# Reordering the projections of a gated-delta mixer and shrinking the fill-in products of the last expert group

## The chip, the core and the metric

The kernel runs on one core of a Trainium2 chip. The metric is the device time of one execution in microseconds; lower is better. The core has five engines that run side by side, each in its own instruction order: PE (TensorE, matrix products), DVE (VectorE), ACT (ScalarE), POOL (GpSimd) and SP (which here issues the loads). An instruction that must wait holds up everything behind it on its engine.

## The reference, cut to what matters

Two model blocks follow each other on 256 tokens of width 1024, in float32. The first block doesn't change here. The second has a mixer and a layer of 64 experts:

```python
def hybrid_mixer(h, ...):                       # h: 16 meta tokens and 256 tokens
    proj = rms_norm_2(h, norm_g) @ w_in
    f_in, qkv, z, ab, gate_f, gate_d = split(proj)
    y_f = fft_mix(f_in) @ w_fourier
    q, k, v = split(silu(depthwise_conv_centred(qkv, conv_w)))     # 5 taps
    q, k = l2_normalize(q), l2_normalize(k)
    o = gated_delta_chunked(q, k, v, g_f, beta_f) + flipped(gated_delta_chunked(flipped ...))
    y_d = (rms_norm_2(o) * silu(z)) @ w_delta
    return (sigmoid(gate_f) * y_f + sigmoid(gate_d) * y_d) @ w_out

def gated_delta_chunked(q, k, v, g, beta):      # per head and chunk
    a_mat = strict_lower(k_beta @ k.T * decay)
    t_mat = inverse(eye + a_mat)                # unit lower triangular
    u, w = t_mat @ (v * beta), t_mat @ (k_beta * exp(g))
    # then a scan over the chunks with a state

def hierarchical_moe(h, ...):                   # 64 experts, 2 per token
    y = (silu(x @ w_gate[e]) * (x @ w_up[e])) @ w_down[e]
```

## The kernel before, in words

**Projections.** Every 128 output features of a projection are one tile: a 512 KB load of float32 weights (`wraw`), a rounded copy `whi` on ACT (L293), the remainder `wlo` on POOL in two halves (L298), and 24 products on PE (`dense_fm`, L333, L334 and L338) into one of four PSUM banks. Then the tile's own `use` function empties the bank. For keys, queries and values it is the convolution (`conv`): a copy on ACT (L1007), four multiply-adds on DVE (L1011), a tanh on ACT (L1013), and a last multiply-add on DVE (L1014). For the gate `gd` it is one tanh on ACT (L1030), for `z` a tanh on ACT (L1038) and one DVE operation (L1039).

**Queue.** The tiles stand in a list, `queue`, in the order in which they were appended: k, q, v, gd, z, f, gf, and `wfo`, eight tiles each for most of them. `fill(n)` emits the next n tiles; `need(label)` emits until none of that label is left.

**Serial work.** Beside the tiles runs the mixer's chain, as generators: `keys` (norms of the keys), `products` (matrices of keys with keys and with queries) beside `meta`, `substitution` (31 dependent steps on DVE that invert 32x32 triangles, L1385 and L1386), `merges` (small products that join the inverted triangles to 128x128), and `scan`. `values` transposes v (L1405, L1406), then makes the start state of the forward scan out of the meta tokens (L1409 to L1425). `weave(gens, per)` steps each generator once, at high priority, then emits `per` tiles. A scheduler with a model of the engines' times then fixes the order on each engine.

```python
weave([products(), meta()], W2)          # 1.3 tiles a round
need("v")
prefetch(NFIX, wst["raw"])               # the first two expert chunks
weave([values(), substitution()], W3)    # 1.0
weave([merges()], W4)                    # 1.0
need("z")
weave([q_factors(), scan(1), scan(0)], W5)
```

**Experts.** The expert weights are 192 chunks of 1 MB, 12 for each of 16 groups of four experts: 8 for gate and up (`gate`, L1783), 4 for down (`down`, L1822). 24 buffers (`slots`) take them; most are tiles of the mixer that have died, so the loads (L888) begin for real when the mixer ends, and a buffer is loaded again as soon as its chunk is used. `combine` (L1836) adds a down product into the result. In the last group, 15, `gate` issues after each chunk one more product of 512 columns that nobody reads (`psidle`, L1786), and `down` one after each of its first three chunks (L1828).

Of the kernel before, what the change touches and what calls it, by code (L numbers as in the profile page):

```python
# [217 lines left out]
def body(ctx, tc, A, out, dbg=None, stage=9):  # L218
# [644 lines left out]
    with b2:  # L863
# [158 lines left out]
        conv("q", 0, NM - 2)  # L1022
        conv("v", 16)

# [16 lines left out]
        for a in range(8):  # L1041
            dense("z", a, NM, use_z)


# [303 lines left out]
        weave([products(), meta()], W2)  # L1348
        need("v")
        prefetch(NFIX, wst["raw"])  # L1350
# [43 lines left out]

        def values():
            G.memset(OT, 0.0)
            for r0 in (0, 64):
                G.memset(Vff[r0 + 32:r0 + 64, F_, r0:r0 + 32], 0.0)
            G.memset(Vff[hi64, F_, lo64], 0.0)
            yield  # L1400
            vm = bp.tile([P, P], F32, name="vm", tag="dm")
            for t in range(2):
# [23 lines left out]

        weave([values(), substitution()], W3)

# [79 lines left out]

        weave([merges()], W4)
        need("z")  # L1510

# [216 lines left out]
    with b3:  # L1728
# [20 lines left out]
        class Four:  # L1749
# [24 lines left out]
            def gate(self, ws, busy=False):  # L1774
                self.ws = ws
                if busy:
                    idle = bank("psidle")
                gu = bank("psgu")
                for k in range(8):
                    if k % 2 == 0:  # L1780
                        self.gather(k // 2 + 2)
                    for q in range(4):
                        PE.matmul(gu[32 * q:32 * q + 32, :], self.xg[:, k, 32 * q:32 * q + 32],  # L1783
                                  ws[k][:, 512 * q:512 * q + 512], start=k == 0, stop=k == 7)
                    if self.g == 15 and busy:
                        PE.matmul(idle, ones, ws[k][:, :512], start=True, stop=True)  # L1786
                a_ = self.act = gp_.tile([P, 256], F32, name="act", bufs=GBUF["act"])
                SC.activation(a_, gu[:, :256], AF.Tanh, scale=0.5)  # L1788
                V.scalar_tensor_tensor(a_, a_, 1.0, gu[:, :256], op0=ALU.add, op1=ALU.mult)  # L1789
                V.scalar_tensor_tensor(a_, a_, 0.5, gu[:, 256:], op0=ALU.mult, op1=ALU.mult)  # L1790
# [23 lines left out]
            def down(self, c, alone=False):  # L1814
# [11 lines left out]
                if self.g == 15 and not alone and c < 3 and BUSY:  # L1826

                    PE.matmul(bank("psidle"), ones, self.ws[8 + c][:, :512], start=True, stop=True)  # L1828
                yh, yl = self.y = [gp_.tile([P, 256], F32R, name=n, bufs=GBUF["y"]) for n in ("yh", "yl")]
# [204 lines left out]
```

## Time and profile before

| | us |
|---|---|
| median of 3 runs | 1176.04 (1172.8 to 1182.49) |
| the profiled execution, its own time | 1175.15 |
| its span from first to last instruction | 1173.4 |
| PE busy in the span | 1056.8 (90%) |
| DVE busy | 545.7 (47%) |
| ACT busy | 437.8 (37%) |
| POOL busy | 426.6 (36%) |

The span falls into the first block (to about 390 us), the mixer (to about 725 us) and the experts (the rest). "Busy" on PE counts waiting inside a pipelined group too, so a full PE row says that the engine had work at hand, not that it ran at its peak. The granted clock of TensorE is given as a share of 2.4 GHz: 1.0 is 2.4 GHz, 0.5 is 1.2 GHz.

### The profile page before, as it was taken

Reading aid. Unit: us, or ns where it says so; the run is one execution under the profiler, and the core shown is the slowest. Engines: PE = TensorE matmul, PEld = TensorE weight load, DVE = VectorE, ACT = ScalarE, POOL = GpSimd, SP = SyncE. Lnnn points to the kernel's source line nnn. Section 1 sums busy time; section 2 is a strip of 40 time slices with the busy share of each in tenths; the row PEclk is TensorE's granted clock in tenths of the full one; section 3 lists DMA queues with packets and bytes.
Section 4 is the critical chain, followed back from the end, with each engine's and each line's share of the span. In section 5 each row is a group of like instructions: output and inputs, shape, how many; then the busy total and the mean of one; then the engine's idle time right before and its main releaser. Section 6 shows DMA issues by size and latency. Waiting matters only on the chain. (4 is left out here: it accounts for less than half of the span.)

```text
span 1173.4 us, 21448 instructions
## 1 busy us (share of the span) xinstructions
PE 1056.8 (90%) x8800; PEld 849.1 (72%) x8800; DVE 545.7 (47%) x1202; ACT 437.8 (37%) x753; POOL 426.6 (36%) x347
## 2 busy tenths in 40 slices
PE   7899999999999979799999999899878778877794
PEld 7899999999998879699999997454424333334351
DVE  5967546433346897885345874222211111112112
ACT  5555435444448455455423553121211111111112
POOL 4565325567773675778545651000000000000100
PEclk9999999999999989899899999999978887888888
DMA  7454434555554323253228798999999999999993
GB/s 285 160 178 160 144 108 168 192 180 180 192 204 163 124 108 108 73 192 145 73 73 316 286 347 325 422 419 421 420 421 420 420 420 420 422 420 421 420 420 118
DMA packets 58858, 307.69 MB, mean 262 GB/s; under 512 B 5984, under 2 KB 7264, under 8 KB 33280
## 3 DMA queue, kind: packets, MB, share of 16 engines
q1 hardware_dynamic: 56528, 301.59, 65.9%
q10 hardware_dynamic: 2224, 4.65, 1.1%
q8 instruction: 71, 1.16, 0.4%
q14 instruction: 35, 0.29, 0.1%
HBM read 304.12 MB, written 2.10 MB: 261 GB/s over the span
## 5 line engine op out<-in xcount | busy, mean ns | idle before, releaser
L298 POOL TENSOR_TENSOR wlo<-wraw,whi 128x512 fp32r<-128x512 f32 x230 | 325.3, 1437 | 233.8 <-ACT whi L293 104.4
L333 PE MATMUL psd<-hTh,whi 128*128 128x256 f32 (+2 forms) x1096 | 275.6, 290 | 5.6 <-ACT whi L293 4.6
L334 PE MATMUL psd<-hTl,whi 128*128 128x256 f32 (+2 forms) x1096 | 274.7, 288 | 2.0 <-DVE hTl L450 1.9
L293 ACT ACTIVATE whi<-wraw 128x1024 fp32r<-128x1024 f32 (+1 forms) x183 | 193.4, 1064 | 200.7 <-PE psd L334 109.1
L333 PEld LDWEIGHTS psd<-hTh,whi 128*128 128x128 f32 x1096 | 210.4, 192 | 8.0 <-ACT whi L293 5.0
L334 PEld LDWEIGHTS psd<-hTl,whi 128*128 128x128 f32 x1096 | 210.9, 193 | 4.4 <-DVE hTl L450 2.8
L1783 PE MATMUL psgu<-wexp,xg 128*32 128x512 f32 x1024 | 146.0, 659 | 41.6 <-DMA wexp<-in_wex_dram 41.5
L338 PE MATMUL psd<-hTh,wlo 128*128 128x256 f32 (+2 forms) x1096 | 159.7, 292 | 0.0
L338 PEld LDWEIGHTS psd<-hTh,wlo 128*128 128x128 f32 x1096 | 145.6, 197 | 1.1 <-issue 0.5
L1971 POOL TENSOR_SCALAR wexp<-cst,gcol 128x128 f32<-128x128 f32 x8 | 4.7, 603 | 387.1 <-PE psgu L1783 387.1
L298 DVE TENSOR_TENSOR wlo<-wraw,whi 128x1024 fp32r<-128x1024 f32 (+1 forms) x68 | 99.7, 1472 | 81.9 <-PE psd L338 61.9
L1783 PEld LDWEIGHTS psgu<-wexp,xg 128*32 128x32 f32 x1024 | 24.8, 112 | 118.2 <-DMA wexp<-in_wex_dram 86.4
L1822 PE MATMUL psy<-wexp,at 128*32 128x256 f32 x1024 | 78.0, 412 | 9.8 <-DVE at L1812 9.2
L1769 PEld LDWEIGHTS psg<-pm,x 128*128 128x128 f32 x512 | 73.6, 223 | 16.6 <-issue 12.0
L1769 PE MATMUL psg<-pm,x 128*128 128x128 f32 x512 | 81.7, 314 | 0.0
L1831 DVE SCALAR_TENSOR_TENSOR yl<-psy,ww,yh 128x256 fp32r<-128x256 f32 x64 | 31.0, 484 | 105.9 <-ACT yh L1830 100.8
L1830 ACT ACTIVATE yh<-psy,ww 128x256 fp32r<-128x256 f32 x64 | 30.3, 474 | 128.2 <-PE psy L1822 122.4
L1789 DVE SCALAR_TENSOR_TENSOR act<-act,psgu 128x256 f32<-128x256 f32 x16 | 6.7, 421 | 135.2 <-ACT act L1788 135.2
L1788 ACT ACTIVATE act<-psgu 128x256 f32<-128x256 f32 x16 | 6.1, 384 | 139.0 <-PE psgu L1783 139.0
L1822 PEld LDWEIGHTS psy<-wexp,at 128*32 128x32 f32 x1024 | 29.5, 114 | 38.4 <-DVE at L1812 13.7
L1771 DVE TENSOR_SCALAR xg<-psg,gcol 128x128 f32<-128x128 f32 x64 | 22.4, 350 | 59.4 <-ACT xg L1770 58.4
L1011 DVE SCALAR_TENSOR_TENSOR ofm<-psd,prm,ofm 128x271 f32<-128x271 f32 (+3 forms) x96 | 44.6, 489 | 9.5 <-ACT ofm L1007 8.5
(641 smaller groups left out, 1619.4 us busy)
## 6 DMA issues: line engine op xcount, KB each, us to landing
wexp<-in_wex_dram SPq DMA_DIRECT2D x191, 1024.0 KB, 19.8
wraw<-in_wf_dram SPq DMA_DIRECT2D x39, 1024.0 KB, 4.9
wraw<-in_wf_dram SPq DMA_DIRECT2D x53, 512.0 KB, 4.4
wraw<-in_wbr_dram SPq DMA_DIRECT2D x8, 1024.0 KB, 5.1
wraw<-in_wtok_dram SPq DMA_DIRECT2D x4, 1160.0 KB, 6.7
wraw<-in_wout_dram SPq DMA_DIRECT2D x4, 1024.0 KB, 4.7
wraw<-in_wde_dram SPq DMA_DIRECT2D x8, 512.0 KB, 6.3
wraw<-in_wo_dram SPq DMA_DIRECT2D x8, 512.0 KB, 7.2
```

Source lines behind the costliest of these rows:

```text
L293: SC.activation(hi, rs, AF.Copy)
L298: eng.tensor_tensor(lo[:, h], rs[:, h], hi[:, h].bitcast(F32), op=ALU.subtract)
L333: PE.matmul(ps, wh[:, ks], part(xh, k, slice(c0, c1)), start=j + k == 0, stop=False, **g)
L334: PE.matmul(ps, wh[:, ks], part(xl, k, slice(c0, c1)), start=False, stop=False, **g)
L338: PE.matmul(ps, wl[:, ks], part(xh, k, slice(c0, c1)), start=False, stop=k == nk - 1, **g)
L1011: V.scalar_tensor_tensor(acc[:, lo:hi], ps[:, lo + d:hi + d], cw(j), acc[:, lo:hi], op0=ALU.mult, op1=ALU.add)
L1769: PE.matmul(ps[:, f], hn[:, t, fs], self.pm[:, t].rearrange("p e c -> p (e c)"), start=t == 0, stop=t == 1)
L1771: V.tensor_scalar(self.xg[:, 2 * f2 + 1], ps[:, 1], gcol[:, 3, 2 * f2 + 1:2 * f2 + 2], None, op0=ALU.mult)
L1783: PE.matmul(gu[32 * q:32 * q + 32, :], self.xg[:, k, 32 * q:32 * q + 32], ws[k][:, 512 * q:512 * q + 512], start=k == 0, stop=k == 7)
L1822: PE.matmul(self.ps[32 * q:32 * q + 32, cs], self.at[:, k, 32 * q:32 * q + 32], self.ws[8 + c][:, o:o + 256], start=k == 0, stop=k == 1)
L1830: SC.activation(yh, self.ps[:, cs], AF.Copy, scale=self.ww)
L1831: V.scalar_tensor_tensor(yl, self.ps[:, cs], self.ww, yh.bitcast(F32), op0=ALU.mult, op1=ALU.subtract)
```

## The change

The value tiles move from third place in the queue, before gd and z, to the place behind z. `need("v")` and `need("z")` go. `values` is split: its clearing of buffers (`zeros`) stays beside the substitution; the rest waits until the last value tile is out of the queue and runs beside the merges. In the last group the fill-in products shrink: in `gate` from 512 to 256 columns, and none behind the last of the eight chunks; in `down` from 512 to 128 columns.

```diff
         conv("k", 8)
         conv("q", 0, NM - 2)
-        conv("v", 16)
...
         for a in range(8):
             dense("z", a, NM, use_z)
+
+        conv("v", 16)
...
         weave([products(), meta()], W2)
-        need("v")
         prefetch(NFIX, wst["raw"])
...
-        def values():
+        def zeros():
             G.memset(OT, 0.0)
             for r0 in (0, 64):
                 G.memset(Vff[r0 + 32:r0 + 64, F_, r0:r0 + 32], 0.0)
             G.memset(Vff[hi64, F_, lo64], 0.0)
             yield
+
+        def values():
+            while pending("v"):
+                yield
             vm = bp.tile([P, P], F32, name="vm", tag="dm")
...
-        weave([values(), substitution()], W3)
+        weave([zeros(), substitution()], W3)
...
-        weave([merges()], W4)
-        need("z")
+        weave([merges(), values()], W4)
...
-                    if self.g == 15 and busy:
-                        PE.matmul(idle, ones, ws[k][:, :512], start=True, stop=True)
+                    if self.g == 15 and busy and k < 7:
+                        PE.matmul(idle[:, :256], ones, ws[k][:, :256], start=True, stop=True)
...
-                    PE.matmul(bank("psidle"), ones, self.ws[8 + c][:, :512], start=True, stop=True)
+                    PE.matmul(bank("psidle")[:, :128], ones, self.ws[8 + c][:, :128], start=True, stop=True)
```

## Rows read from the trace of the kernel before

**Rows 1.** The page: span, and GB/s moved in 40 equal slices.
```profile
span 1173.4 us, 21448 instructions
...
GB/s 285 160 178 160 144 108 168 192 180 180 192 204 163 124 108 108 73 192 145 73 73 316 286 347 325 422 419 421 420 421 420 420 420 420 422 420 421 420 420 118
```

**Rows 2.** Chain that ended last, in order of time: start, length, what.
```profile
726.86 0.99 PE psgu L1783 x8
...
812.26 1.00 PE psgu L1783 x8
813.80 19.81 DMA wexp<-in_wex_dram
...
1095.21 19.86 DMA wexp<-in_wex_dram
...
1130.55 1.00 PE psgu L1783 x8
1131.54 1.06 PE psidle L1786 x2
```

**Rows 3.** Busy time by stretch: length, engines (instructions), granted PE clock, DMA share, GB/s.
```profile
486.00:494.00 8.00, 1.59 (x6) 0.90 (x5) 7.96 (x12) 2.69 (x3) 8.00 (x5) 0.77 0.40 131
494.00:501.00 7.00, 6.43 (x30) 6.43 (x31) 6.28 (x26) 3.13 (x6) 3.03 (x3) 0.53 0.01 4
...
520.00:540.00 20.00, 20.00 (x172) 20.00 (x171) 17.79 (x22) 9.53 (x16) 17.17 (x17) 1.00 0.75 288
...
560.00:570.00 10.00, 10.00 (x71) 9.52 (x71) 3.12 (x6) 5.85 (x10) 4.55 (x4) 0.56 0.29 107
...
600.00:620.00 20.00, 20.00 (x179) 20.00 (x178) 6.13 (x10) 5.62 (x7) 8.73 (x7) 1.00 0.14 53
```

**Rows 4.** Waits of PE, 455 to 600 us: total, times, longest.
```profile
PE psv L1405 <- DVE qk L1307: 5.5, 1, 5.5
```

**Rows 5.** Groups by line, 455 to 580 us: busy us, mean ns, idle before.
```profile
L1011 DVE SCALAR_TENSOR_TENSOR ofm<-psd,prm,ofm 128x270 f32<-128x270 f32 (+3 forms) x36 | 17.1, 492 | 2.8 <-ACT ofm L1007 2.4
...
L1039 DVE SCALAR_TENSOR_TENSOR sz<-th,psd 128x256 f32<-128x256 f32 x8 | 3.2, 416 | 8.0 <-ACT th L1038 7.9
L1030 ACT ACTIVATE sgd<-psd 128x256 f32<-128x256 f32 x8 | 2.9, 367 | 0.6 <-PE psd L338 0.6
```

**Rows 6.** Timeline, DVE then PE: last substitution step, last merge copy, first scan product.
```profile
536.65 1.16 DVE L1386 TENSOR_REDUCE X<-xt 128x31 f32<-128x961 f32 x1
...
574.70 1.23 DVE L1492 COPY An<-W 64x1024 f32<-64x1024 f32 x1 [0.47 <-PE W L1488]
...
577.69 0.38 PE L1549 MATMUL psvn<-vb,An 128*128 128x128 f32 x2
```

**Rows 7.** Timeline of the values' steps on PE, ACT and POOL: start, length, what.
```profile
510.95 1.04 PE L1405 MATMUL psv<-cst,vr 128*128 128x128 f32 x8
...
512.02 1.03 ACT L1406 ACTIVATE v<-psv 128x1024 f32<-128x1024 f32 x1 [0.69 <-PE psv L1405]
...
536.69 1.90 POOL L1419 TENSOR_TENSOR vbl<-vnm,cst 128x1024 f32<-128x1024 f32 x1 [0.34 <-PE psd L334]
...
541.27 1.88 PE L1423 MATMUL pS<-vbl,kdm 128*128 128x512 f32 x4
```

**Rows 8.** PE timeline: gate of group 14, then gate and down of group 15.
```profile
1107.66 1.93 PE L1783 MATMUL psgu<-wexp,xg 128*32 128x512 f32 x8 [0.54 <-DMA wexp<-in_wex_dram]
...
1112.63 1.07 PE L1783 MATMUL psgu<-wexp,xg 128*32 128x512 f32 x8 [0.73 <-DMA wexp<-in_wex_dram]
...
1145.87 1.06 PE L1783 MATMUL psgu<-wexp,xg 128*32 128x512 f32 x8
...
1149.41 1.07 PE L1822 MATMUL psy<-wexp,at 128*32 128x256 f32 x16 [0.56 <-ACT rs_ready L185]
...
1156.76 1.07 PE L1822 MATMUL psy<-wexp,at 128*32 128x256 f32 x16
```

**Rows 9.** Busy time by stretch behind the last load (columns as in rows 3).
```profile
1152.00:1154.00 2.00, 2.00 (x22) 0.91 (x12) 0.31 (x1) 0.82 (x4) 0.00 (x0) 1.00 0.00 0
```

## The prediction

> **What bounds the kernel now.** I read the page first, to see which resource is full in which part. The slices of GB/s [rows 1] show two regimes: below 320 GB/s up to slice 21, and 419 to 422 in slices 26 to 39 without a dent. So from about 733 us the kernel is bound by the expert weights. The chain of waits [rows 2] says how that stretch is fed: from the first gate product at 726.86 to 812.26 us PE works off chunks that lie ready, from 813.80 to beyond 1095.21 the chain is nothing but loads, and at the end it is PE again. The pace of the loads is read from two gate steps of group 14 that waited for them: 1107.66 and 1112.63 are two chunks apart, (1112.63 - 1107.66) / 2 = 2.49 us each [rows 8]. 24 of the 192 chunks are in buffers when the experts begin, and 168 x 2.49 = 418 us are left; from 726.86 to the end of the loads before 1152 us [rows 9] it is 425. The stream can't be shortened, only moved: every microsecond by which the mixer ends earlier frees buffers earlier and moves first gate, stream and end by the same. What else can be gained is behind the stream's end.
>
> Next the mixer in stretches [rows 3]. PE has work all the time in 520 to 540 and 600 to 620 us, with 172 and 179 products in 20 us, 0.11 to 0.12 us each. It doesn't in 486 to 494: 1.59 of 8 us busy, DVE 7.96 of 8. In 494 to 501 it works, but at a granted clock of 0.53, nearly the lower level of 1.2 GHz. The waits name the hold-up [rows 4]: the transposes of v (`psv`) stand at PE's head for 5.5 us, because their PSUM buffer waits for a DVE operation of `products`. DVE has a backlog there, and part of it is the convolution of v.
>
> **Cost of the order, part by part.** The diff adds and removes no work in the mixer; it moves it, so the price of each part is what it stood in the way of.
>
> Value tiles out of the products. One tile's convolution costs DVE four operations of 0.492 us [rows 5] and a last one of about the same: 2.4 us, 19 us for eight tiles. The tiles that take their place leave DVE alone: gd needs 0.367 us of ACT, z needs ACT and 0.416 us of DVE [rows 5]. So a PSUM bank of gd is free again as soon as ACT gets to it, and PE has tiles to work on while DVE does `products`. The `psv` transposes are gone from that place too. Lost before: 8.00 - 1.59 = 6.4 us of standstill in 486 to 494. Behind it, 6.43 us of work at a clock of 0.53, which at the full clock is 6.43 x 0.53 = 3.4 us: 3.0 lost [rows 3]. Together 9.4 us. Bound below: nothing, if the same wait only moves to the next product that needs DVE. Bound above: 9.4 us, and the 6 us that convolutions of v took from DVE inside the first third of the substitution (an estimate: twelve operations of 0.49), 15 us. I take the 9.4.
>
> Value tiles beside the merges. They are now the last eight of 24 tiles before the scan. Four of them, by the count of fills (11 rounded in `products`, 9 in `substitution`, then one a round), come behind the substitution. There DVE has room: 3.12 of 10 us busy in 560 to 570 [rows 3]. But DVE takes things in order, and the merges wait for five copies on it; I charge each of them with one convolution operation that it finds ahead of it, 5 x 0.49 = 2.4 us. Lower bound 0, if the merges' priority holds; upper bound all four tiles in the way, 4 x 2.4 = 9.6 us. I take 2.4, near the lower end, because in 520 to 540, where DVE was full, the substitution's steps still went ahead of the tiles.
>
> The values' chain. It ran under the substitution, whose last step began at 536.65; now it begins with the last value tile. The backward scan needs v only: two transposes and two copies, 2 x (1.04 + 1.03) = 4.1 us [rows 7], and a scaled copy on POOL of the size of `vbl`, 1.90 us: 6 us. The forward scan needs the start state: `vbl` 1.90, `pS` 1.88, its copy about 1.03, and five small steps between, an estimate of 2 us: 4.1 + 6.8 = 11 us. Before, the merges ended with a copy at 574.70 + 1.23 and the scan's first product came at 577.69 [rows 6]. If the last value tile is emptied 6 us before the merges end, it is free for the backward scan; the forward scan starts up to 5 us late, and other tiles (five of f and gf, emitted during the values' rounds) keep PE busy meanwhile. I take 0, with 5 and 11 as the ends of the rival below.
>
> `need("v")`, `need("z")`: 0. z is now ahead of v, so the wait for v includes it. The two chunks of `prefetch` are issued some tiles earlier on SP's queue, two loads of 2.49 us among tiles whose DMA share is 0.01 to 0.40 there [rows 3]: 0; at worst the tile loads behind them come 5 us late once, as they would have before.
>
> Mixer: -9.4 + 2.4 = -7.0 us, moved in full to the end.
>
> **Cost of the fill-in products.** A gate step of group 15 now takes 1.00 + 1.06 = 2.06 us [rows 2], less than a chunk's 2.49; but the group begins late. Chunk 7 of its gate, 12 behind the one used at 1112.63 [rows 8], lands at 1112.63 + 12 x 2.49 = 1142.5, and is used at 1145.87: PE is 3.4 us behind. With half the columns (0.53, an estimate from the 1.06) seven steps save 7 x 0.53 = 3.7, so PE catches up with the load to within its own 1.5 us step: 3.4 saved. In `down`, the way from the last gate step to the first down product, 1149.41 - 1145.87 = 3.54, stays, and contains the dropped eighth product, off the way. From the first to the last down product there are 1156.76 - 1149.41 = 7.35 us with three fill-ins; three quarters of three are 3 x 0.8 = 2.4 us. But the last chunk is in only shortly before 1152 [rows 9], so the last down product can move from 1156.76 to 1152 at most, 4.8 us. 3.4 + 2.4 = 5.8 exceeds that; with a step or so of slack I take -4.0. Ends: -4.8, and the clock's price below. What is late next is the last chunk itself.
>
> **Sum.** Span 1173.4 - 7.0 - 4.0 = 1162.4; the profiled execution is 1.75 us longer than its span, 1164.15, and lies 0.9 us under the median of the runs. I predict 1164 us. One per cent is about what a measurement of this kernel can tell from no change: it is 1164.3 below and 1187.8 above.
>
> **Rivals.**
>
> *The values come late* (the other side). Mechanism: DVE works on the substitution without a gap, and value convolutions are pushed behind it or, emitted before its end, between its steps. Then their banks fill, PE stands as it did in 486 to 494, and the last value tile is emptied only when the merges are done. Price: 6 us for the backward and 11 us for the forward scan, on average 8.5, and the 9.4 gained are stood out again. 1175.15 + 8.5 - 4.0 = 1180; with the upper 9.6 on the merges too, 1189. It decides when the last value tile is emptied later than 6 us before the last merge copy. For it: DVE was busy 17.79 of 20 us in 520 to 540 [rows 3]. Against it: 3.12 of 10 us in 560 to 570. Chance 0.14.
>
> *Only the tail.* PE's hold-up moves to another DVE wait of `products`, nothing more: 1175.15 - 4.0 = 1171. For it: the transposes of `meta` wait for DVE in the same place. Chance 0.18.
>
> *More than the hold-up.* The substitution starts and ends earlier by DVE's 6 us, and the merges' stretch at a clock of 0.56 in 560 to 570 [rows 3], where tiles now fill PE better, gets some of its 4.4 us back: 1175.15 - 15 - 4 = 1156. For it: DVE was the full engine before the merges. Against it: the small products of the merges stay. Chance 0.15.
>
> *The clock falls in the last group.* Group 14, which has no fill-in products, shows the price: a gate step of 1.93 us at 1107.66 against 1.07 at 1112.63 [rows 8]. At the lower level a step of group 15 would take 1.93 + 1.06 = 2.99, above 2.49; four such steps lose 2 us, and four down steps of about 1.9 more each lose 7: against before about +5 instead of -4, with the mixer's gain 1175.15 - 7 + 5 = 1173. Against it: PE, 3.4 us behind, still runs without a gap through most of the gate. Chance 0.08. The Trainium skill, "TensorE: Matmul & The Clock Gate", Part 1, makes the lower clock the default that activity has to lift, which speaks against smaller fill-in products; by it this rival would be the rule wherever PE waits for loads. Here the trace agrees only in part: the gate of group 14 shows both levels under the same waits.
>
> **How the numbers follow.** My forecast has 0.45, its own range is 1158 to 1170 (mixer -13 to -2 with the tail at -4). 8 times in 10: the two rivals of 1171 and 1173 lie inside, the one of 1156 at the lower edge; up to the near half of the late values, 1180. So 1156 to 1180. Faster by over 1%, below 1164.3: 0.27 of my forecast's 0.45 and the 0.15 of the large gain, 0.42. Slower by over 1%: the upper half of the late values, 0.07. Within 1%: 0.51.
>
> **What would show it.** Right: in the stretch before the substitution PE busy without the 5.5 us wait of `psv`, and a clock of 1.0; the last substitution step before 530; the first scan product near 571; the first gate near 720; gate steps of group 15 at 1.5 us that end by waiting for a load; the last down product within 1 us of the last load. Wrong: a scan product that waits for `vb` or `krl`; DVE's convolutions of v between the substitution's steps; DMA below 400 GB/s once the experts run; a clock of 0.5 in the last group.

## The result: slower by 1.1%, where 1% faster was forecast

The changed kernel takes 1189.11 us (median of 4 runs, 1188.69 to 1190.48), the kernel before beside it 1174.43 us; the ratio is 1.0111, 95% interval 1.0068 to 1.0154. The prediction was 1164 us with a range of 1156 to 1180: the time lies outside, on the other side. The profiled execution of the changed kernel took 1189.12 us, its span is 1187.3 us.

The page of the changed kernel, span and GB/s in 40 slices [rows 1]:

```profile
span 1187.3 us, 21441 instructions
GB/s 281 158 163 172 143 107 178 180 204 182 181 178 160 157 72 107 118 249 73 72 72 216 292 343 319 367 412 421 420 420 421 421 420 420 421 421 421 420 420 166
```

The stream of the expert weights is what it was, 412 to 421 GB/s in slices 26 to 38. First gate product to the last load is 1169 - 743.0 = 426 us, against 425 before. So the loss lies ahead of the first gate product: 743.0 us, 16.2 later than the 726.86 of [rows 2].

Busy time of the changed kernel in four of the stretches of [rows 3], same columns:

```profile
486.00:494.00 8.00, 7.29 (x59) 6.77 (x57) 7.15 (x21) 4.26 (x6) 8.00 (x5) 1.00 0.39 133
494.00:501.00 7.00, 5.36 (x36) 4.54 (x37) 5.31 (x20) 2.66 (x4) 7.00 (x6) 1.00 0.30 63
520.00:540.00 20.00, 15.99 (x124) 15.31 (x122) 19.92 (x30) 9.79 (x14) 16.96 (x14) 1.00 0.72 274
600.00:620.00 20.00, 17.08 (x147) 16.46 (x145) 17.65 (x27) 6.33 (x11) 16.04 (x13) 1.00 0.23 77
```

The hold-up did go: 7.29 of 8 us busy in 486 to 494 where it was 1.59, and a clock of 1.00 in both of the first rows. But 520 to 540, where PE had work throughout, is now DVE's (19.92 of 20), and PE has 124 products in place of 172.

The merges' products come in the order Z', W', Z, W (`Zp`, `Wp`, `Z`, `W` in the rows); a scan product is a row `psvn`. The mixer's end in stages, from 440 us to the first reduction of the substitution, to the first Z' product, to the first scan product, to the transposes of the output, to the first gate product. First the kernel before, then the changed kernel (columns as in rows 3):

```profile
440.00:495.30 55.30, 48.32 (x338) 43.45 (x338) 43.24 (x106) 29.14 (x41) 38.27 (x30) 0.93 0.28 96
495.30:544.00 48.70, 48.70 (x382) 47.63 (x380) 43.71 (x92) 25.15 (x38) 38.03 (x36) 0.95 0.51 180
544.00:577.70 33.70, 32.23 (x598) 31.09 (x598) 9.27 (x12) 15.08 (x21) 18.87 (x16) 0.80 0.28 96
577.70:653.60 75.90, 74.45 (x633) 74.25 (x632) 41.15 (x91) 31.47 (x49) 42.25 (x43) 0.98 0.51 191
653.60:726.80 73.20, 72.18 (x587) 69.12 (x586) 50.66 (x124) 35.62 (x60) 33.11 (x28) 1.00 0.83 320
```

```profile
440.00:491.10 51.10, 50.62 (x381) 46.58 (x380) 31.87 (x82) 28.17 (x39) 34.75 (x27) 0.97 0.26 86
491.10:540.30 49.20, 42.74 (x332) 40.52 (x331) 43.86 (x96) 21.14 (x32) 44.65 (x42) 1.00 0.61 218
540.30:598.40 58.10, 56.04 (x740) 52.29 (x741) 27.02 (x45) 25.20 (x37) 26.86 (x33) 0.79 0.16 56
598.40:671.10 72.70, 67.43 (x582) 66.64 (x581) 47.18 (x86) 27.37 (x42) 37.08 (x29) 1.00 0.58 221
671.10:743.00 71.90, 64.78 (x502) 61.00 (x502) 45.17 (x117) 31.73 (x57) 25.38 (x23) 0.98 0.77 290
```

In stage lengths: 55.3 to 51.1, 48.7 to 49.2, 33.7 to **58.1**, 75.9 to 72.7, 73.2 to 71.9. The stage of the merges alone is 24.4 us longer; the rest gives 8.2 back. The timelines of `psd` count the dense products of the projections (L333, L334, L338 on `hTh` and `hTl`) in the five stages as 220, 347, 85, 266, 192 before and 258, 319, 180, 158, 192 after: as many in all but for three, 108 of them moved from the scan's stage, mostly into the merges'. The other products of these lines (on `fhl`) moved up in turn: 14 in the scan's stage and 84 behind it before, 96 and none after. Of the 24.4 us, 5.5 are a lower clock: 0.21 x 58.1 = 12.2 us lost against 0.20 x 33.7 = 6.7.

What stood in the merges' stage, in order of time (start, length, what, [idle before <- released by]); compare [rows 6, 7]:

```profile
535.25 1.14 DVE L1386 TENSOR_REDUCE X<-xt 128x31 f32<-128x961 f32 x1
...
570.35 0.44 DVE L1014 SCALAR_TENSOR_TENSOR vr<-psd,ofm 128x272 f32<-128x272 f32 x1 [1.43 <-ACT psd L1013]
572.10 0.38 PE L1409 MATMUL psv<-cst,vr 128*128 128x128 f32 x2
572.41 1.94 ACT L1410 ACTIVATE v<-psv 128x1024 f32<-128x1024 f32 x2 [2.10 <-PE psv L1409]
573.49 0.68 PE L1480 MATMUL Z<-ofm,An 64*64 64x64 f32 x8 [0.90 <-ACT v L1410]
...
574.51 0.30 ACT L1413 ACTIVATE vm<-pst 128x128 f32<-128x128 f32 x1
581.00 0.63 PE L1419 MATMUL pst<-vm,XRm 128*128 128x128 f32 x2
583.01 1.89 POOL L1423 TENSOR_TENSOR vbl<-vnm,cst 128x1024 f32<-128x1024 f32 x1
...
587.02 1.90 POOL L1533 TENSOR_TENSOR vb<-v,be 128x1024 f32<-128x1024 f32 x1 [2.08 <-PE psrq L1508]
...
594.28 1.23 DVE L1496 COPY An<-W 64x1024 f32<-64x1024 f32 x1 [4.22 <-PE W L1492]
594.63 1.88 PE L1427 MATMUL pS<-vbl,kdm 128*128 128x512 f32 x4
596.55 1.03 ACT L1429 ACTIVATE krl<-pS 128x1024 f32<-128x1024 f32 x1 [8.77 <-PE pS L1427]
598.35 0.83 PE L1552 MATMUL psvn<-vb,An 128*128 128x128 f32 x6
```

The substitution's last step is at 535.25, 1.4 us earlier than in [rows 6]; it started 4.2 us earlier. v's last tile is emptied at 570.35 + 0.44. The values and the merges share two two-bank PSUM buffers, and Z's products come only when the first of v's two copies frees one (the row of L1480, released by `v`): at 573.49, 10.5 us later than in the kernel before:

```profile
L1476 PE MATMUL Z<-ofm,An x32: 311/311/366, 563.0 to 566.3; 64*64 64x64 f32 x32
```

PE itself stood for only 0.90 us of that; it had dense products to work on. And between the steps of the values' chain lie gaps in which the next step waits for its turn in PE's order: vm is there at 574.81, its product comes at 581.00; `vbl` is there at 584.90, `pS` comes at 594.63. `krl`, the first state, is copied at 596.55 to 597.58, and the first scan product follows at 598.35 instead of 577.69. That product is the backward scan's and reads `vb` and `An`, not the state. Both are there before (588.92 and 595.51), and PE has no idle time just ahead of it: it comes in its turn, behind `pS` and dense products.

The last group, PE's timeline, and busy time about the last load [rows 8, 9]:

```profile
1147.60 1.07 PE L1786 MATMUL psgu<-wexp,xg 128*32 128x512 f32 x8
1148.59 0.70 PE L1789 MATMUL psidle<-wexp,ones 128*128 128x256 f32 x2
...
1153.50 1.07 PE L1786 MATMUL psgu<-wexp,xg 128*32 128x512 f32 x8
1155.13 1.07 PE L1786 MATMUL psgu<-wexp,xg 128*32 128x512 f32 x8
...
1163.55 1.07 PE L1825 MATMUL psy<-wexp,at 128*32 128x256 f32 x16 [0.56 <-ACT rs_ready L185]
1170.51 1.07 PE L1825 MATMUL psy<-wexp,at 128*32 128x256 f32 x16 [0.63 <-DVE yl L1834]
```

```profile
1168.00:1170.00 2.00, 1.87 (x22) 1.01 (x14) 1.02 (x4) 1.07 (x6) 0.00 (x0) 1.00 0.13 53
1170.00:1172.00 2.00, 1.49 (x20) 0.91 (x20) 1.12 (x3) 0.66 (x4) 0.00 (x0) 1.00 0.00 0
```

Gate steps of 1.62 to 1.63 us at the full clock, the last load in at 1169, the last down product at 1170.51. From 1169 to the span's end are 18 us, from the last load of the kernel before ([rows 9]) 21.4.

### The profile page after: what moved, and what is told of

It is laid out like the page before. It is cut to its first block, busy times and chain, and to the rows that moved or that the text cites. A ratio compares the mean times of both kernels' runs of the same rounds, so it can differ in the third digit from the quotient of the medians.

```text
span 1187.3 us, 21441 instructions
## 1 busy us (share of the span) xinstructions
PE 1060.6 (89%) x8798; PEld 852.3 (72%) x8798; DVE 552.7 (47%) x1202; ACT 434.7 (37%) x751; POOL 422.3 (36%) x347
## 4 chain that ended last, share of the span: by engine, by line
DMA 27%; PE 20%; DVE 8%; ACT 2%; issue 1%; POOL 1%; ACTq 0%; SPq 0%; DVEq 0%
DMA wexp<-in_wex_dram 25%; PE psgu L1786 3%; PE psy L1825 2%; PE psg L1772 2%; PE psd L333 2%; PE psd L334 2%; PE psd L338 1%; PE acc L1839 1%; DVE ofm L1011 1%; DMA wraw<-in_wo_dram 1%; POOL wlo L298 1%; DMA wraw<-in_wde_dram 1%; DVE X L1386 1%; ACT whi L293 1%; DVE xt L1385 1%
## 5 line engine op out<-in xcount | busy, mean ns | idle before, releaser
L298 POOL TENSOR_TENSOR wlo<-wraw,whi 128x512 fp32r<-128x512 f32 x230 | 323.5, 1430 | 226.7 <-ACT whi L293 119.1
L333 PE MATMUL psd<-hTh,whi 128*128 128x256 f32 (+2 forms) x1096 | 280.8, 293 | 10.2 <-ACT whi L293 5.3
L334 PE MATMUL psd<-hTl,whi 128*128 128x256 f32 (+2 forms) x1096 | 279.0, 292 | 3.5 <-DVE hTl L450 3.0
L333 PEld LDWEIGHTS psd<-hTh,whi 128*128 128x128 f32 x1096 | 214.1, 196 | 14.0 <-ACT whi L293 6.7
L334 PEld LDWEIGHTS psd<-hTl,whi 128*128 128x128 f32 x1096 | 214.5, 196 | 6.0 <-DVE hTl L450 4.2
L1786 PE MATMUL psgu<-wexp,xg 128*32 128x512 f32 x1024 | 148.6, 669 | 38.1 <-DMA wexp<-in_wex_dram 38.0
L338 PE MATMUL psd<-hTh,wlo 128*128 128x256 f32 (+2 forms) x1096 | 157.0, 288 | 1.1 <-POOL wlo L298 1.1
L338 PEld LDWEIGHTS psd<-hTh,wlo 128*128 128x128 f32 x1096 | 142.4, 192 | 3.0 <-POOL wlo L298 2.0
L298 DVE TENSOR_TENSOR wlo<-wraw,whi 128x1024 fp32r<-128x1024 f32 (+1 forms) x68 | 97.9, 1446 | 80.5 <-PE psd L338 63.4
L1772 PEld LDWEIGHTS psg<-pm,x 128*128 128x128 f32 x512 | 76.2, 230 | 16.9 <-issue 12.3
L1772 PE MATMUL psg<-pm,x 128*128 128x128 f32 x512 | 84.1, 321 | 0.0
L1011 DVE SCALAR_TENSOR_TENSOR ofm<-psd,prm,ofm 128x270 f32<-128x270 f32 (+3 forms) x96 | 44.7, 489 | 13.3 <-ACT ofm L1007 12.2
```

What stands on the lines that cost most here:

```text
L298: eng.tensor_tensor(lo[:, h], rs[:, h], hi[:, h].bitcast(F32), op=ALU.subtract)
L333: PE.matmul(ps, wh[:, ks], part(xh, k, slice(c0, c1)), start=j + k == 0, stop=False, **g)
L334: PE.matmul(ps, wh[:, ks], part(xl, k, slice(c0, c1)), start=False, stop=False, **g)
L338: PE.matmul(ps, wl[:, ks], part(xh, k, slice(c0, c1)), start=False, stop=k == nk - 1, **g)
L1011: V.scalar_tensor_tensor(acc[:, lo:hi], ps[:, lo + d:hi + d], cw(j), acc[:, lo:hi], op0=ALU.mult, op1=ALU.add)
L1772: PE.matmul(ps[:, f], hn[:, t, fs], self.pm[:, t].rearrange("p e c -> p (e c)"), start=t == 0, stop=t == 1)
```

## The experiments

Four theories came up in turn. **1**: v's transposes hold both two-bank PSUM buffers while they wait for late v tiles. **2**: the late v tiles themselves, and the chain behind them. **3**: dense products in the merges' stage cost PE time that they didn't cost in the scan. **4**: the values' chain stands beside the merges and not beside the substitution.

**The last group alone.** The kernel before with

```
-                    if self.g == 15 and busy:
-                        PE.matmul(idle, ones, ws[k][:, :512], start=True, stop=True)
+                    if self.g == 15 and busy and k < 7:
+                        PE.matmul(idle[:, :256], ones, ws[k][:, :256], start=True, stop=True)
...
-                    PE.matmul(bank("psidle"), ones, self.ws[8 + c][:, :512], start=True, stop=True)
+                    PE.matmul(bank("psidle")[:, :128], ones, self.ws[8 + c][:, :128], start=True, stop=True)
```

> The kernel before, with the two edits of the last group's fill-in products alone. Theory 1 (the last group gained what the prediction's sum said, and the mixer lost more than that): 1170 to 1171 us, 3.6 to 4.0 us under the kernel before; from the last load to the end 17.5 to 18 us instead of 21.4; the mixer's steps where the kernel before has them (first scan product within 1 us of 577.7, first gate within 2 us of 726.9). Rival (the last group's gain hangs on the later arrival of its work in the new order): no gain, within 1 us of the kernel before.

Measured: 1170.01 us against 1176.98, ratio 0.9956 (0.9922 to 0.9991), which is 5.2 us, 1 to 9; first scan product 575.8, first gate 724.9. From the last load to the end are about 18 us, from the first gate to the end 443.4, against 446.6 in the kernel before. So the profile gives the last group 3.2 us; the gain is real and doesn't need the new order. This kernel beats both.

**The order alone.** The changed kernel with the old fill-in products.

> The changed kernel with the old fill-in products of the last group, that is the new order of the mixer's work alone. Theory 1: first scan product near 598, first gate near 743, and the tail of the kernel before; so 3.6 to 4 us over the changed kernel, about 1193 us, 18 us over the kernel before. Rival (the fill-in products are what costs, somewhere in the last groups): at most 1180 us.

Measured: 1189.99 us, ratio 1.0134 (1.0082 to 1.0185); first scan product 594.8, first gate 740.4. From the first gate to the end of the span 447.9 us, against 444.3 in the changed kernel: the 3.6 us of the last group are there, hidden in the times by a mixer that was 2.6 us faster in this run. The order is what costs.

**The values behind the merges.**

```
-        weave([merges(), values()], W4)
+        weave([merges()], W4)
+        weave([values()], W4)
```

> The changed kernel with the merges first and the values behind them, each with its own share of the dense tiles, in place of the two in turns. Theory 1 (the values' transposes hold both two-bank PSUM buffers of the tag s while they wait for late v tiles, so that Z's second product waits 10.5 us for a buffer): Z's second product follows the last copy of W' within 3 us (near 563 instead of 573.5), the first scan product is 5 to 12 us earlier than 598, and the time is 1177 to 1184 us. Rival A (the v tiles themselves are late, whatever holds the buffers): Z's second product is early, but the values' chain (their transposes, copies and decays) now follows it, the first scan product stays at 596 to 604 and the time within 5 us of 1189. Rival B (the cost is the convolution's vector work between the steps): the wait for the buffer goes, another for VectorE takes its place, and the time is within 3 us of 1189.

Measured: 1193.55 us, ratio 1.0158 (1.0093 to 1.0224). Last copy of the merges, v's last tile, its copies, first state's copy, first scan product:

```profile
568.96 1.23 DVE L1496 COPY An<-W 64x1024 f32<-64x1024 f32 x1 [0.47 <-PE W L1492]
579.95 0.44 DVE L1014 SCALAR_TENSOR_TENSOR vr<-psd,ofm 128x272 f32<-128x272 f32 x1 [1.33 <-ACT psd L1013]
580.96 1.94 ACT L1410 ACTIVATE v<-psv 128x1024 f32<-128x1024 f32 x2 [1.04 <-PE psv L1409]
606.13 1.03 ACT L1429 ACTIVATE krl<-pS 128x1024 f32<-128x1024 f32 x1 [5.10 <-PE pS L1427]
L1553 PE MATMUL psvn<-vb,An x16: 272/275/275, 607.7 to 609.4; 128*128 128x128 f32 x16
```

The PSUM wait is gone and the merges end at 570.2, 25 us earlier than in the changed kernel. Nothing is won: the values end 27 us behind v's last tile (580.4 to 607.2), the same 27 as in the changed kernel (570.8 to 597.6). Theory 1 falls as the cause; the wait was real, but not what held up the scan last. The first scan product is 3.7 us beyond the bound of rival A.

**No multiply-adds for v, order of before.** `for j in (0, 1, 3, 4) if n != "v" else ():` at L1008 in the kernel before.

> The kernel before without four of the five multiply-adds of the convolution for the values alone (that part of the computation is left out; everything else is kept). It takes the vector work away that fed the hold-up ahead of the substitution, and puts it nowhere else. The prediction's step (9.4 us of hold-up that reach the end): psv waits at most 1 us, the substitution's last step near 527, the first scan product near 568, and 1165 to 1168 us. Theory 1's reading (the relief is given back by other vector work between the substitution's steps, which was moved there): the same, since here nothing is moved there. Rival (the hold-up was hidden: PE fills it with dense tiles that are due later anyway): the substitution begins earlier, but the first gate moves by less than 4 us and the time stays at 1171 to 1176.

Measured: 1167.31 us against 1176.98, ratio 0.9963 (0.9927 to 0.9998). Last step of the substitution 532.1, first scan product 569.1, first gate 717.9, 8.9 us earlier than in the kernel before; the span is 8.3 us shorter. PE in the stage ahead of the substitution:

```profile
440.00:491.00 51.00, 50.49 (x377) 46.44 (x376) 33.46 (x85) 31.83 (x46) 34.90 (x28) 1.00 0.27 92
```

0.5 us of idle time at a clock of 1.00, where the kernel before has 7.0 us at 0.93. In this stage the relief is 6.5 us of idle time and 3.9 of clock, about what the prediction's first term said (9.4). How much of it reaches the end is less sure. Within the substitution 3.2 us of idle time come back, and 3.3 of the 8.9 us at the first gate are a higher clock in the merges' stage (0.89 against 0.80), which the kernel with the last group alone has too. The ratio of times gives 4.4 us, 0.2 to 8.6.

**v's tiles ahead of z's.** `conv("v", 16)` moved ahead of the loop over z, in the changed kernel.

> The changed kernel with one thing moved in the queue of dense tiles: the eight tiles of v before the eight of z, not behind them. The run with the values behind the merges freed the two-bank PSUM buffers and brought no time back, so theory 2 takes the place of theory 1: v's last tile is emptied at 570.8 us, and its chain (transposes, copies, memory row, decayed copy, first state) needs 27 us behind it (570.8 to 597.6, and 580.4 to 607.2 with the values behind the merges), whatever the merges do. Theory 2 expects here: all v tiles emptied within the substitution, by 540; the substitution 3 to 8 us longer, since three more tiles' vector work falls between its steps; Z' from 543 to 549; the first scan product 33.7 us behind it as in the kernel before, 577 to 583; first gate 725 to 732; 1170 to 1178 us. Rival B (the values' vector work between the steps is the cost, wherever its tiles stand): substitution longer by as much as the merges gain, first scan product at 592 or later, 1184 us or more. Rival C (z is what the end waits for): first scan product early, first gate still at 740 or later.

Measured: 1208.21 us, ratio 1.0256 (1.0194 to 1.0317). v is emptied by 534.8, as intended, but the substitution now has the vector work of all eight v tiles between its steps: its last step is at 547.5 (535.3 in the changed kernel). The W' products, in turns with dense products, reach from 565.1 to 590.2 (550.4 to 557.1 in the changed kernel), at a clock of 0.73 over the whole stage, and the first scan product comes at 618.8. Earlier v tiles alone don't help; theory 2 in its plain form falls. The numbers are those of rival B, which the next run tests.

**The new order without the multiply-adds for v.**

> The changed kernel without four of the five multiply-adds of the convolution for the values (that part of the computation is left out). Theory 2 (the tiles' place in the queue and the 27 us behind them): the substitution ends 7 to 9 us earlier, near 527, but v's last tile still comes after it, with the merges, and its chain behind it; first scan product 584 to 592, and 1175 to 1184 us, so 10 us or more over the kernel before without the same multiply-adds (1167.3 us, first scan product at 569.1). Rival B (the vector work is the cost of the new order): with that work gone the new order costs nothing; first scan product at 570 or earlier, and 1160 to 1167 us.

Measured: 1189.28 us, ratio 1.0116 (1.0071 to 1.0161). The substitution's last step comes at 530.1, 5.2 us earlier, the first scan product at 587.9; the first gate at 740.5, 2.5 us earlier than in the changed kernel. The first scan product lies where theory 2 has it, the time 5 us above its bound. With the vector work out of both orders, the new one is still 18 (by the two ratios) to 22 us (by the medians) slower, even with the last group's gain on its side (1189.3 against 1167.3, first gate 740.5 against 717.9). The vector work between the steps is not the cost.

**v's tiles first.** The changed kernel with `conv("v", 16)` right behind `conv("q", 0, NM - 2)`.

> The changed kernel with the tiles of v back at the kernel before's place in the queue, behind q and ahead of gates and z; the substitution doesn't wait for them (the need for v ahead of it stays out) and the values stay woven with the merges. Theory 2: the last v tile is emptied early in the substitution, the values' chain lies under the substitution and the merges; no hold-up of PE ahead of the substitution over 2 us; first scan product 570 to 578; 1164 to 1172 us. Rival B (the vector work that leaves the hold-up comes back between the substitution's first steps): last step of the substitution at 536 or later, first scan product 576 to 580, and within 2 us of the kernel before with the new fill-in products alone (1170 us). Rival D (the PSUM buffers: the values' transposes, now in the merges' weave, hold them against the merges even when v is early): Z's second product waits over 4 us for a copy of v, and the first scan product is at 580 or later.

Measured: 1181.29 us, ratio 1.0063 (1.0031 to 1.0095). v is complete at 505.7 (504.8 before), but no expectation came true as a whole. The hold-up ahead of the substitution is back: PE stands 7.1 us for a step of `meta` (`pst`, L1331, waiting for DVE's `XRm`), though the transposes of v are gone from there. So, with the run without multiply-adds, it was v's vector work that fed it, and not the transposes. Z waits for no copy of v. v's memory row (its part for the meta tokens, `mst`) is collected at once; PE's transpose of it, the last copy of the merges, the first state's product and the first scan product:

```profile
L1217 POOL COPY mst<-vr x1: 238/238/238, 506.3 to 506.3; 128x64 f32<-128x64 f32 x1
L1219 PE MATMUL pst<-cst,mst x1: 270/270/270, 577.5 to 577.5; 128*128 128x128 f32 x1
577.08 1.23 DVE L1496 COPY An<-W 64x1024 f32<-64x1024 f32 x1 [1.71 <-PE W L1492]
L1427 PE MATMUL pS<-vbl,kdm x4: 590/592/592, 589.1 to 590.4; 128*128 128x512 f32 x4
L1552 PE MATMUL psvn<-vb,An x16: 270/275/275, 592.4 to 594.1; 128*128 128x128 f32 x16
```

The row is ready at 506.5 and PE gets to it at 577.5; in the kernel before these two are 506.8 and 532.0. The merges end at 578.3, the scan starts 14 us later. This kernel differs from the kernel with the last group alone in little but the place of the values, and is 11 us slower (1181.3 against 1170.0): theory 4.

**How many dense products stand in the merges' stage.** Four runs at theory 3, with one constant each: W4 (dense tiles per step of the merges' weave) 0.5 in the changed kernel; W4 0.5 in the kernel with v first; W4 0 in the kernel with the last group alone; and 1.6 for W3 at the substitution's weave in the changed kernel.

> The changed kernel with one constant changed: half a dense tile is handed out per step of the merges and the values (W4 = 0.5 in place of 1.0). In PE's order this leaves 100 dense products between the first Z' product and the first scan product, where the changed kernel has 180 and the kernel before 84; what is left of them stands in the scan (236, against 156 and 264). Theory 3, from the runs so far: that stretch is full of PE work in every kernel (96% busy), so each dense product more in it costs 0.24 to 0.25 us (before 85 products in 33.7 us, first-in-line values 169 in 48.9, changed kernel 180 in 58.1, values behind the merges 226 in 66.6), while in the scan and the output that follow, a chain of 143 to 149 us whatever PE is given, the same products are free. Theory 3 expects 35 to 40 us for the stretch, first scan product at 575 to 581, first gate at 720 to 727, 1167 to 1174 us. Theory 2 (the values' 27 us behind the last v tile decide): v's last tile at 560 or later as in the changed kernel, first scan product at 588 or later, 1180 us or more.

> The run with v's tiles first (behind q, no need for v ahead of the substitution) with W4 = 0.5 in place of 1.0: 102 dense products between the first Z' product and the first scan product where that run had 169, 221 in the scan where it had 155. Theory 3: the stretch shrinks from 48.9 us to 33 to 38, first scan product at 577 to 582, first gate at 721 to 727, 1166 to 1173 us. Rival (what costs there is the values' chain in the merges' weave, not the dense products): first scan product stays within 4 us of 592, the time within 4 us of 1181.

> The kernel before with the new fill-in products of the last group, and W4 = 0 in place of 1.0: nothing of the order of keys, queries, substitution and values is changed, but PE's order now has 113 dense products between the first Z' product and the first scan product in place of 84, and 235 in the scan in place of 264. Theory 3: the stretch grows by 29 x 0.24 = 7 us, from 30.4 to 33.7 us to 37 to 41; the scan gets nothing back; first gate 5 to 8 us later than the 724.9 of the same kernel with W4 = 1.0, 1174 to 1180 us against 1170.0. Rival (moved dense products are neutral, since PE does them once in either place): within 2 us of 1170.

> The changed kernel with 1.6 dense tiles handed out per step of the substitution in place of 1.0: v's tiles are asked for earlier, and PE's order has 240 dense products between the first Z' product and the first scan product (180 in the changed kernel) and 96 in the scan (156). Theory 3: the stretch is 60 x 0.24 = 14 us longer than 58.1 us, 68 to 74, first scan product 606 to 620 and 1195 to 1212 us. Theory 2 (late v): v's tiles are asked for earlier, so the first scan product is earlier than 598 and the time under 1187 us.

Measured, in the same order: 1192.9 us (ratio 1.0123, 1.0077 to 1.0169), 1174.55 (0.9993, 0.9966 to 1.002), 1186.99 (1.0099, 1.0068 to 1.013) and 1188.61 (1.0107, 1.0059 to 1.0154). Two of the four speak against theory 3: with 100 products the stage still took 51.3 us, and with 240 it took 62.0, not 68 to 74, and the first gate came at 740.9, not later than in the changed kernel. The run with v first agrees in direction and falls short in size: 41.6 us for the stage, not 33 to 38, and 1.5 us above the bound of 1173. In the kernel with W4 0, fewer tiles asked for left more products in the stage (113). The stage took 40.8 us, within the theory's 37 to 41. But 14.8 us went at the first gate (739.7 against 724.9), of which the theory had 7: 10.4 in this stage and 4.8 behind the scan. So tiles that change places can cost almost as much as the new order did, with the values' chain where it was. The first of the four beside the run with v first, which has as many products (busy time from first Z' to first scan product):

```profile
541.10:592.40 51.30, 48.31 (x652) 43.28 (x653) 21.87 (x41) 21.62 (x32) 23.11 (x27) 0.70 0.18 63
```

```profile
542.50:584.10 41.60, 40.46 (x654) 36.72 (x654) 11.31 (x15) 18.45 (x27) 23.07 (x23) 0.88 0.19 69
```

652 and 654 instructions, a clock of 0.70 and of 0.88: 51.3 and 41.6 us.

**The values early, everything else as changed.** The changed kernel with

```
-            while pending("v"):
-                yield
...
-                    PE.transpose(ps[:, h], row("v", h)[:, NM + t * P:NM + t * P + P], ident)
+                    PE.transpose(ps[:, h], row("q", h)[:, NM + t * P:NM + t * P + P], ident)
...
-            ps = meta_rows("v")
+            ps = meta_rows("q", NM)
...
-            yield
+            sub["vbl"], sub["kdm"] = vbl, kdm
+
+        def state():
+            vbl, kdm = sub["vbl"], sub["kdm"]
+            while pending("v"):
+                yield
             ps = big("pS0")
...
-        weave([zeros(), substitution()], W3)
+        weave([zeros(), values(), substitution()], W3)
...
-        weave([merges(), values()], W4)
+        weave([merges(), state()], W4)
```

> The changed kernel, its tiles in its own order (v behind gates and z, with all of v's vector work), but the values' chain reads q's rows in place of v's and so runs beside the substitution as in the kernel before; only its last step (first state, two products' worth of PE time and a 1.03 us copy) stays with the merges and still waits for v's tiles. The values' part of the result is therefore computed from the wrong rows; every instruction of it is there. What the runs so far say: theory 3 (each dense product between the first Z' product and the scan costs 0.24 us) fell with W4 = 0.5 (100 products, still 51.3 us) and with 1.6 tiles per step of the substitution (240 products, and no slower than the changed kernel). In seven kernels with the values beside the merges the first scan product follows the copy of the first state by about 1 us, and in six of them that copy comes 2 to 37 us behind the last copy of the merges; in the four with the values beside the substitution it follows the merges. Theory 4: the values' chain is what the scan waits for, because it stands beside the merges and not beside the substitution. It expects here that the scan is released by the merges or within 3 us of them: first scan product 570 to 582, first gate 721 to 731, 1167 to 1178 us. Rival (v's tiles and their vector work between the substitution's steps and the merges cost the time, whatever the values' chain does): first scan product at 588 or later, 1183 us or more.

Measured: 1167.48 us against 1175.4, ratio 0.9918 (0.9891 to 0.9946). v's last tile, the first state's copy, the last copy of the merges, the first scan product:

```profile
568.94 0.44 DVE L1014 SCALAR_TENSOR_TENSOR vr<-psd,ofm 128x272 f32<-128x272 f32 x1 [0.64 <-ACT psd L1013]
570.93 1.02 ACT L1432 ACTIVATE krl<-pS 128x1024 f32<-128x1024 f32 x1
580.58 1.23 DVE L1499 COPY An<-W 64x1024 f32<-64x1024 f32 x1 [0.47 <-PE W L1495]
L1555 PE MATMUL psvn<-vb,An x16: 271/275/275, 584.5 to 588.0; 128*128 128x128 f32 x16
```

v's tiles are as late as in the changed kernel (568.94 against 570.35), and here it costs nothing: the state is there 2.6 us behind the last tile, the merges end last, the first scan product comes 13.9 us and the first gate 19.0 us earlier (724.0). The first scan product is 2.5 us later than theory 4 expected; the rest is within its bounds, and the rival's 1183 is out. Late v tiles, their vector work between the steps and z ahead of v are all in this kernel, so none of them costs the time by itself. What costs is the values' chain standing in the merges' stage. The two belong together, though: this kernel takes its values from the wrong rows, which are there earlier, and with the right ones the chain can't start before v's tiles. The chain's place costs 11 us with v first and 22 us with v late.

**PE's account.** Where the 19 us lie is best seen as PE time. From 440 us to the first gate product the length is PE's idle time, the time that a lower clock lost ((1 - granted clock) x length, stage by stage), and the rest:

| kernel | length | idle | lost clock | rest | first scan product | first gate |
|---|---|---|---|---|---|---|
| before | 286.8 | 10.9 | 14.6 | 261 | 577.7 | 726.8 |
| last group alone | 284.9 | 10.2 | 11.8 | 263 | 575.8 | 724.9 |
| before, no multiply-adds for v | 277.9 | 7.1 | 6.8 | 264 | 569.1 | 717.9 |
| changed | 303.0 | 21.4 | 15.2 | 266 | 598.4 | 743.0 |
| values behind the merges | 307.2 | 26.8 | 15.2 | 265 | 607.7 | 747.2 |
| v first | 296.2 | 19.5 | 13.3 | 263 | 592.4 | 736.2 |
| changed, W4 0.5 | 305.8 | 18.4 | 22.5 | 265 | 592.4 | 745.8 |
| v ahead of z | 320.7 | 23.4 | 25.9 | 271 | 618.8 | 760.7 |
| values early | 284.0 | 9.4 | 10.8 | 264 | 584.5 | 724.0 |

The rest is nearly the same, here and in the other five kernels: 261 to 266 us, but for one. Single traces are only so exact: kernels with the same mixer differ by 1.9 us (before, last group alone) and 2.6 us (changed, order alone) at the first gate. The work is a fixed amount of PE time, and what can be won or lost is idle time and clock. The new order gained 6.5 us of idle time ahead of the substitution (7.0 to 0.5) and lost 6.5 in it (0 to 6.5), 0.6 in the merges, 3.8 in the scan and 6.1 behind it. The tiles that PE worked off earlier were missing later, while it served the chains. Of the 16.2 us by which the first gate is later, 10.5 are idle time, 0.6 clock and 5.1 the rest. Of the 19.0 between the changed kernel and the one with the values early, 12.0 are idle time, 4.4 clock and 2.6 the rest. How much of this comes from the chain's turns, and how much from the dense products that its place displaces, the runs don't separate.

## Why the prediction was wrong, point by point

**The hold-up ahead of the substitution: gone, as forecast, but its worth at the end was overrated.** 7.3 of 8 us are busy at a clock of 1.00, without the wait of [rows 4]. The term of 9.4 us was taken as moved to the end in full. In the changed kernel the 6.5 us of idle time gained come back as 6.5 us within the substitution. With the values early 6.8 are gained and 4.9 come back, and the first gate is 2.8 us earlier than in the kernel before, where the forecast had 7.0.

**"The last substitution step before 530": wrong.** It began 4.2 us earlier and ended 1.4 earlier. Fourteen convolution operations of 0.4 to 0.5 us came between its steps from 522.9 on; 520 to 540 shows DVE at 19.92 of 20 us. The prediction had listed this as a sign of being wrong, and counted the operations in its sum only at the merges. It isn't the cost, though: without four fifths of that work the new order was no faster.

**"Value tiles beside the merges", 2.4 us: not found.** Six of v's tiles, not four, were emptied behind the substitution. But DVE was idle ahead of all five copies that the prediction charged (L1467, L1469, L1471, L1494, L1496), until ACT or PE was done.

**"The values' chain: I take 0": the step that failed.** The prediction added up the durations of its steps, 11 us at most, and let it begin with the last v tile beside merges that end when they always ended. Measured, it takes 27 us behind the last tile, of which 6.2 (574.8 to 581.0) and 9.7 (584.9 to 594.6) are its steps waiting for their turn in PE's order, behind dense products and those of the merges; its transposes take the PSUM buffers that Z wants; the merges' stage, with 95 more dense products in it, gets 24 us longer. That PE was full there is in the kernel before's own stage row: 32.2 of 33.7 us busy between first Z' and first scan product. A chain of PE steps put into a stage where PE is full took its turns, not its durations. Taken out again, with all else as changed, 21.6 us came back (1189.1 to 1167.5).

**"Moved in full to the end": right.** 16.2 us at the first gate are 13.9 at the span's end, with the last group's gain between them; the stream takes 426 us, before 425.

**The last group: right.** -4.0 forecast; 3.6 between the changed kernel and the order alone; by itself 3.2 in the profile and 5.2 (1 to 9) in the times. Gate steps took 1.62 us instead of the forecast 1.5 and didn't come to wait for loads, since the group began behind; the last down product came 1.5 us behind the last load, not within 1. The clock did not fall.

**The rivals.** "The values come late" had the right place and 1180 to 1189; that 1189.1 is its upper end is partly luck. Its mechanism was only half right: banks didn't fill, the hold-up did not come back, and its condition (last v tile under 6 us ahead of the last merge copy) wasn't met, 570.8 against 595.5; the merges were late with it. It deserved more than 0.14. "Only the tail" had the hold-up move to another DVE wait; that is seen with v first (7.1 us), not in the changed kernel. With the values early, the kernel takes 1167.5, inside the forecast's own 1158 to 1170. But its ratio of 0.9918 (0.9891 to 0.9946) and that of the last group alone, 0.9956 (0.9922 to 0.9991), overlap: what the rest of the new order adds to the last group's gain isn't clear of noise, and the -7.0 us for the mixer is not shown.

Open is why the scan and what follows are 5 us shorter with the values early (139.5 us from first scan product to first gate against 144.6): PE's idle time there is 3.4 us against 12.4, but no single wait accounts for it. Open is also which part of the loss goes to the clock of the merges' stage. A form in which only the memory row's steps leave the merges was not tried.

## What to carry to other kernels

When a dependent chain is moved, price it by the turns of the busiest in-order engine in its new stage, not by the sum of its own durations: count the chain's steps on that engine, and what stands queued between them. Ask of each stage whether that engine is full there; a chain that fits into one stage can wait for its turns in the next, and tiles used up early are missing later. And try independent parts of a change apart: here one was a gain that the other hid.

## What the runs showed of the hardware

**The same products at two speeds.** The merges' stage with 652 and 654 instructions ran at a granted clock of 0.70 and 0.88 (rows above), and over all runs from 0.70 to 0.93, between the two levels of 1.2 and 2.4 GHz. PE was busy 0.94 and 0.97 of the time in these two. Ahead of the low stretches stand the merges' small products: in the changed kernel the dense products right behind the 32 by 32 ones of Z', 545.1 to 548 us, are one per 0.22 to 0.23 us, those from 548.5 on one per 0.12. Over the runs it took 3 to 17 us from this stage, as much as the effects that were looked for. What sets it off, no run here shows.

**DVE standing behind POOL.** A step of the other branch on DVE mostly takes 0.22 us, and once 4.45 (DVE, then POOL, changed kernel):

```profile
580.54 4.45 DVE L1067 TENSOR_TENSOR krl<-ofm 128x69 f32<-128x69 f32 x1 [3.00 <-POOL krl L1064]
584.91 0.22 DVE L1068 TENSOR_TENSOR krl<-ofm 128x69 f32<-128x69 f32 x1
```

```profile
580.51 2.50 POOL L298 TENSOR_TENSOR wlo<-wraw,whi 128x512 fp32r<-128x512 f32 x2
583.01 1.89 POOL L1423 TENSOR_TENSOR vbl<-vnm,cst 128x1024 f32<-128x1024 f32 x1
```

It begins with two operations of POOL (L298, together 2.50 us) and ends at 584.99, just behind a third (L1423, 1.89 us, to 584.90). The Trainium skill, "SBUF — State Buffer", section "Who interferes with whom", has the two engines share a pair of ports as an exclusive lock, the loser blocked; this row agrees, and suggests that the loser can stand behind several operations in a row. That the ports are the reason is read from these times alone; no run tests it. PE had no idle time then.
